# A convolution on one Trainium2 core: all input loads issued at the start, the first store held until the sixth of seven has landed

## The chip, the core and the metric

The kernel runs on one core of a Trainium2 chip. The time is device microseconds of one execution, given as the median of several runs. Before the change it is 125.88 us, the median of three runs (125.75 to 125.93).

## What is computed

```python
x: (16, 64, 64, 64) float32        # batch, c_in, h, w
weight: (128, 64, 3, 3) float32    # 90% of its entries are zero
x_pad = pad(x, 1 pixel of zeros on each side of h and w)
output[b, co] += weight[co, ci, kh, kw] * x_pad[b, ci, kh:kh+64, kw:kw+64]   # over ci, kh, kw
```

It is an ordinary 3x3 convolution with padding 1. The output is (16, 128, 64, 64) float32. The kernel uses the weights as a dense matrix. HBM gives 16.78 MB of x and 0.29 MB of weights, and takes 33.55 MB of output; the profile counts 17.07 MB read and 33.55 MB written.

## The kernel before

**Pairs.** The 16 images are worked on in eight pairs, p = 0 to 7. A pair's two images lie on 128 partitions (2 x 64 input channels) in one bf16 tile `xs[p]` of 64 x 64 pixels. All eight tiles stay in SBUF. The loads run on POOL's DMA queue (L63 and `load`, L68) and cast float32 to bf16 on the way, so a full load reads 2.10 MB of HBM and writes 1.05 MB into SBUF; the profile lists it as 1024 KB. Only the upper 32 rows of pair 0 come differently: SP's queue loads them as float32 into `x_head` (L62), and DVE and ACT cast them (L101). The weights are the first transfer of SP's queue (L60).

**Work on a pair.** A pair is cut into four blocks of 16 rows. Except for the very first block (`direct`), a block goes through `twos` (L166). POOL adds each even row to the odd row below it (`s`, L169, a pool of three buffers). PE multiplies that sum (6 matmuls; L150), and ACT copies the product out of PSUM into `pc` (L176). Then PE computes what the even rows lack (12 matmuls), and DVE adds it to `pc` and writes the result into the output tile `o` (L183, two instructions), then the same for the odd rows. PSUM has eight tiles (`psum_pool`), and a block uses six of them. The two images' matmuls run on different halves of the array.

**Outputs.** `o` is a tile of 128 x 2 x 64 x 64 float32 (4.19 MB, one pair of output images), from a pool of three buffers. SP's queue stores a whole pair when its last block is done (L207), and pair 7 in two halves (L205). Pair 3 writes into the buffer of pair 0, pair 4 into that of pair 1, and so on, so DVE's first write of pair p waits for the store of pair p-3 to land.

**Order.** The schedule is by hand (`tc.manual_schedule()`): each engine does its instructions in the order of the program, and the framework adds the waits on semaphores. POOL's order counts twice, since its loads and its additions `s` are in one stream. Before the change POOL issues, ahead of its first `s`, the tail of pair 0, pairs 1 to 3 and the first 24 rows of pair 4. The rest follows behind the last block of a pair:

```python
EARLY, CUT = 4, 24
LATER = {2: (5,), 3: (6,), 4: (7, 0, 32), 5: (7, 32, 64)}
```

After pair 1 comes the rest of pair 4 (L197), after pair 2 pair 5, after pair 3 pair 6, after pairs 4 and 5 the two halves of pair 7 (L199). After the store of pair 1, SP issues five transfers of 4 bytes (`spare`, L211). Their data is never used; each takes the next semaphore of the eight that SP's transfers use in turn.

Of the kernel before, what the change touches and what calls it, by code (L numbers as in the profile page):

```python
# [8 lines left out]
FP32 = mybir.dt.float32  # L9
# [2 lines left out]
SUB = mybir.AluOpType.subtract  # L12

BLOCKS = {p: "TTTT" for p in range(8)}
BLOCKS[0] = "DTTT"  # L20


G0, G1, G2, G21, G01 = range(5)
# [4 lines left out]
def kernel(  # L28
# [6 lines left out]
    nc = tc.nc  # L35

    B, C_IN, H, W = x.shape
    C_OUT, _, KH, KW = weight.shape
    assert (B, C_IN, H, W) == (16, 64, 64, 64) and (C_OUT, KH, KW) == (128, 3, 3)
    NP = B // 2  # L40
    HEAD = 32

    const_pool = ctx.enter_context(tc.tile_pool(name="const", bufs=1))
    x_pool = ctx.enter_context(tc.tile_pool(name="x", bufs=1))
    s_pool = ctx.enter_context(tc.tile_pool(name="s", bufs=3))
    p_pool = ctx.enter_context(tc.tile_pool(name="pc", bufs=4))
    o_pool = ctx.enter_context(tc.tile_pool(name="o", bufs=3))
    psum_pool = ctx.enter_context(
        tc.tile_pool(name="psum", bufs=8, space=bass.MemoryType.PSUM)
    )  # L50
# [4 lines left out]
    def pair(p):  # L55
        return x[2 * p : 2 * p + 2].rearrange("n i h w -> (n i) h w")

    xs = [x_pool.tile([128, H, W], BF16, name=f"x{p}") for p in range(NP)]
# [5 lines left out]
    ident = const_pool.tile([128, 128], BF16, name="ident")  # L64
    make_identity(nc, ident)

    def load(p, a=0, b=H):
        nc.gpsimd.dma_start(out=xs[p][:, a:b, :], in_=pair(p)[:, a:b, :])  # L68

    EARLY, CUT = 4, 24

    LATER = {2: (5,), 3: (6,), 4: (7, 0, 32), 5: (7, 32, 64)}
    for p in range(1, EARLY):
        load(p)
    load(EARLY, 0, CUT)


    idle_rhs = const_pool.tile([128, 512], BF16, name="idle_rhs")  # L80
    nc.vector.memset(idle_rhs, 0.0)  # L81
# [2 lines left out]
    def keep_busy(n):  # L84
        for _ in range(n):
            nc.tensor.matmul(idle_ps, idle_rhs[:, 0:128], idle_rhs, start=True, stop=True)  # L86

    keep_busy(7)

    w_v = w_sb.rearrange("o (i k) -> o k i", k=KH * KW)
# [66 lines left out]
    def direct(p, o, r0, rows):  # L159
        ps = product(  # L160
            [(xs[p], G1, r0, 1), (xs[p], G0, r0 - 1, 1), (xs[p], G2, r0 + 1, 1)], rows
        )
        nc.scalar.copy(out=o[0][:, r0 : r0 + rows, :], in_=ps[0])  # L163
        nc.vector.tensor_copy(out=o[1][:, r0 : r0 + rows, :], in_=ps[1])  # L164

    def twos(p, o, r0):  # L166
        t0 = r0 // 2
        s = s_pool.tile([128, 8, W], BF16, name="s")
        nc.gpsimd.tensor_tensor(  # L169
            out=s, in0=xs[p][:, r0 : r0 + 16 : 2, :], in1=xs[p][:, r0 + 1 : r0 + 16 : 2, :], op=ADD  # L170
        )
        shared = product([(s, G1, 0, 1)], 8)
        pc = []
        for n in range(2):
            c = p_pool.tile([128, 8, W], FP32, name="pc")
            nc.scalar.copy(out=c, in_=shared[n])  # L176
            pc.append(c)
        even = [(xs[p], G21, r0 + 1, 2), (xs[p], G0, r0 - 1, 2)]
        odd = [(xs[p], G01, r0, 2), (xs[p], G2, r0 + 2, 2)]
        for first, terms in ((r0, even), (r0 + 1, odd)):  # L180
            ps = product(terms, 8)
            for n in range(2):
                nc.vector.tensor_tensor(  # L183
                    out=o[n][:, first : r0 + 16 : 2, :], in0=ps[n], in1=pc[n], op=ADD
                )

    for p in range(NP):
        both = o_pool.tile([C_OUT, 2, H, W], FP32, name="o")
        o = [both[:, n] for n in range(2)]
        into = out[2 * p : 2 * p + 2].rearrange("n o h w -> o n h w")  # L190
        last = p == NP - 1
        for blk in range(4):
            r0 = 16 * blk
            if BLOCKS[p][blk] == "T":
                twos(p, o, r0)
                if p == 1 and blk == 3:
                    load(EARLY, CUT, H)  # L197
                elif blk == 3 and p in LATER:
                    load(*LATER[p])  # L199
            else:  # L200
                for r, rows in ((r0, 8), (r0 + 8, 8)):
                    direct(p, o, r, rows)
            if last and blk % 2 == 1:
                rows = slice(r0 - 16, r0 + 16)
                nc.sync.dma_start(out=into[:, :, rows, :], in_=both[:, :, rows, :])  # L205
        if not last:
            nc.sync.dma_start(out=into, in_=both)  # L207
        if p == 1:
            spare = const_pool.tile([1, 5], FP32, name="spare")
            for k in range(5):  # L210
                nc.sync.dma_start(out=spare[:, k : k + 1], in_=weight[0:1, 0, 0, 0:1])  # L211


# [28 lines left out]
```

## Time and profile before

| | |
|---|---|
| time, median of 3 runs | 125.88 us (125.75 to 125.93) |
| span of the profiled execution | 124.3 us, so 1.5 us of the time lie outside the span |
| PE busy | 108.7 us (87%) |
| DVE busy | 82.5 us (66%) |
| ACT and POOL busy | 39.0 and 41.7 us |
| shares of the 16 DMA engines: SP's queue q1, POOL's queue q0 | 67.2% and 30.7% |
| stores issued by SP (pairs 0 to 6, then the two halves of 7) | 23.03, 35.78, 48.58, 61.39, 74.19, 87.00, 99.81; 106.16 and 112.61 us |

The profile shows one execution, in microseconds from the first instruction. A page of it gives the busy time of each engine, rows of 40 slices for engines and DMA, the queues, the chain of work that ended last, the groups of instructions, and the DMA issues with their time to landing. "SPq" and "POOLq" are the DMA queues that SP and POOL fill: q1 (called hardware_dynamic) and q0 (software_dynamic). "Landing" is when the transfer's semaphore reports it complete.

One column needs care. The bytes of q0 are those written into SBUF as bf16. A casting load reads twice as many bytes from HBM, so q0's megabytes are doubled below wherever a rate at the HBM is meant.

### The profile page before, as it was taken

Reading aid. Unit: us, or ns where it says so; the run is one execution under the profiler, and the core shown is the slowest. Engines: PE = TensorE matmul, PEld = TensorE weight load, DVE = VectorE, ACT = ScalarE, POOL = GpSimd, SP = SyncE. Lnnn points to the kernel's source line nnn. Section 1 sums busy time; section 2 is a strip of 40 time slices with the busy share of each in tenths; the row PEclk is TensorE's granted clock in tenths of the full one; section 3 lists DMA queues with packets and bytes.
Section 4 is the critical chain, followed back from the end, with each engine's and each line's share of the span. In section 5 each row is a group of like instructions: output and inputs, shape, how many; then the busy total and the mean of one; then the engine's idle time right before and its main releaser. Section 6 shows DMA issues by size and latency. Waiting matters only on the chain.

```text
span 124.3 us, 2453 instructions
## 1 busy us (share of the span) xinstructions
PE 108.7 (87%) x989; PEld 57.2 (46%) x989; DVE 82.5 (66%) x135; ACT 39.0 (31%) x71; POOL 41.7 (34%) x47
## 2 busy tenths in 40 slices
PE   6959999999999999999999999999999999970000
PEld 2425555555555555555555555555555555530000
DVE  0353577877787778777877878887877787772000
ACT  4543333333333333333333333333333333330000
POOL 6409333533353335333443335333333320000000
PEclk9999999999999999999999999999999999997555
DMA  4999999999999999999999999999999999999991
GB/s 120 348 220 227 219 213 213 238 411 338 335 392 422 319 316 324 377 340 329 303 385 378 354 380 443 376 349 389 418 422 437 422 427 427 437 427 403 432 414 82
DMA packets 4198, 42.91 MB, mean 345 GB/s; under 512 B 347, under 2 KB 347, under 8 KB 1115
## 3 DMA queue, kind: packets, MB, share of 16 engines
q1 hardware_dynamic: 2746, 34.90, 67.2%
q0 software_dynamic: 1440, 7.86, 30.7%
q8 instruction: 7, 0.11, 0.3%
q14 instruction: 5, 0.03, 0.1%
HBM read 17.07 MB, written 33.55 MB: 407 GB/s over the span
## 4 chain that ended last, share of the span: by engine, by line
PE 82%; DMA 5%; DVE 1%; issue 1%; DVEq 0%; SPq 0%
PE ps L150 82%; DMA x_head<-in_x_dram 5%; DVE o L183 1%; DVEq L237 0%; DVE x L101 0%; SPq L60 0%; DVEq L183 0%
## 5 line engine op out<-in xcount | busy, mean ns | idle before, releaser
L183 DVE TENSOR_TENSOR o<-ps,pc 128x512 f32<-128x512 f32 x124 | 77.8, 686 | 22.1 <-PE ps L150 19.2
L150 PE MATMUL ps<-x,wT 64*128 64x504 bf16 (+3 forms) x780 | 88.8, 373 | 1.3 <-DVE x L101 1.3
L150 PEld LDWEIGHTS <-wT 64*128 64x128 bf16 x966 | 55.2, 94 | 49.5 <-issue 1.7
L169 POOL TENSOR_TENSOR s<-x 128x512 bf16<-128x512 bf16 x31 | 35.6, 1150 | 57.6 <-PE ps L150 41.1
L176 ACT COPY pc<-ps 128x512 f32<-128x512 f32 x62 | 33.3, 589 | 64.0 <-issue 61.8
L150 PE MATMUL ps<-s,wT 64*128 64x512 bf16 (+1 forms) x186 | 25.7, 377 | 0.0
L86 PE MATMUL ps<-idle_rhs 128*128 128x512 bf16 x14 | 4.8, 505 | 1.2 <-DVE idle_rhs L81 1.2
L68 POOL DMA_DIRECT2D x<-in_x_dram x9 | 5.0, 560 | 0.0
L86 PEld LDWEIGHTS <-idle_rhs 128*128 128x128 bf16 x14 | 1.5, 118 | 3.2 <-issue 1.4
L105 DVE CAST w_bf<-w_sb 128x192 bf16<-128x192 f32 (+1 forms) x4 | 1.1, 351 | 2.5 <-DMA w_sb<-in_weight_dram 2.5
L164 DVE COPY o<-ps 128x512 f32<-128x512 f32 x2 | 1.4, 692 | 2.0 <-PE ps L150 2.0
L101 DVE CAST x<-x_head 128x576 bf16<-128x576 f32 x1 | 0.5, 460 | 2.6 <-DMA x_head<-in_x_dram 2.6
L101 ACT CAST x<-x_head 128x576 bf16<-128x576 f32 (+1 forms) x2 | 1.5, 802 | 1.8 <-DMA x_head<-in_x_dram 1.8
L163 ACT COPY o<-ps 128x512 f32<-128x512 f32 x2 | 1.2, 586 | 2.4 <-PE ps L150 2.4
L105 ACT ACT_TABLE_LOAD x1 | 1.3, 1283 | 0.7 <-PEq L226 0.7
L105 ACT CAST w_bf<-w_sb 128x64 bf16<-128x64 f32 (+1 forms) x2 | 0.7, 416 | 1.6 <-DMA w_sb<-in_weight_dram 1.6
L115 DVE TENSOR_TENSOR wT<-ps,wT 128x384 bf16<-128x384 f32 x2 | 1.0, 548 | 0.0
L111 PEld LDWEIGHTS <-w_bf 128*128 128x128 bf16 x9 | 0.5, 97 | 1.0 <-DVE w_bf L105 1.0
L63 POOL DMA_DIRECT2D x<-in_x_dram x1 | 0.7, 693 | 0.8 <-POOLq L226 0.8
L111 PE MATMUL ps<-ident,w_bf 128*128 128x128 bf16 x9 | 0.9, 222 | 0.1
L81 DVE MEMSET idle_rhs<- 128x256 uint32 x1 | 0.3, 272 | 0.9 <-PEq L226 0.9
L126 DVE CAST wT<-ps 128x384 bf16<-128x384 f32 x1 | 0.6, 551 | 0.0
(8 smaller groups left out, 1.9 us busy)
## 6 DMA issues: line engine op xcount, KB each, us to landing
out_dram<-o SPq DMA_DIRECT2D x7, 4096.0 KB, 19.8
x<-in_x_dram POOLq DMA_DIRECT2D x5, 1024.0 KB, 16.8
out_dram<-o SPq DMA_DIRECT2D x2, 2048.0 KB
x<-in_x_dram POOLq DMA_DIRECT2D x3, 512.0 KB, 13.8
x_head<-in_x_dram SPq DMA_DIRECT2D x1, 1024.0 KB, 6.2
x<-in_x_dram POOLq DMA_DIRECT2D x1, 640.0 KB, 14.8
x<-in_x_dram POOLq DMA_DIRECT2D x1, 384.0 KB, 22.3
w_sb<-in_weight_dram SPq DMA_DIRECT2D x1, 288.0 KB
```

Source lines behind the costliest of these rows:

```text
L68: nc.gpsimd.dma_start(out=xs[p][:, a:b, :], in_=pair(p)[:, a:b, :])
L86: nc.tensor.matmul(idle_ps, idle_rhs[:, 0:128], idle_rhs, start=True, stop=True)
L101: copy(out=xs[0][:, a:b, :], in_=x_head[:, a:b, :])
L105: copy(out=w_bf4[:, g, a:b, :], in_=w_v[:, k : k + b - a, :])
L111: nc.tensor.matmul(wps[:, j, :], src, ident, start=True, stop=True)
L115: nc.vector.tensor_tensor(out=wT[:, g], in0=wps, in1=wT[:, G1], op=SUB)
L150: nc.tensor.matmul(ps[n][:, lo:hi, c_lo:c_hi], tap(g, kw, n), src[q, a:b:step, c_lo + kw - 1 : c_hi + kw - 1], start=(i == 0), stop=(i == ...
L163: nc.scalar.copy(out=o[0][:, r0 : r0 + rows, :], in_=ps[0])
L164: nc.vector.tensor_copy(out=o[1][:, r0 : r0 + rows, :], in_=ps[1])
L169: nc.gpsimd.tensor_tensor(out=s, in0=xs[p][:, r0 : r0 + 16 : 2, :], in1=xs[p][:, r0 + 1 : r0 + 16 : 2, :], op=ADD)
L176: nc.scalar.copy(out=c, in_=shared[n])
L183: nc.vector.tensor_tensor(out=o[n][:, first : r0 + 16 : 2, :], in0=ps[n], in1=pc[n], op=ADD)
```

## The change

The loads of pairs 1 to 7 are all issued at the beginning, each as one transfer, and none later. The store of the first half of pair 0 additionally waits for the load of pair 6 (`loads[5]`, the sixth of the seven). The stores of pairs 0 and 1 are cut into halves, as that of pair 7 was. The three output buffers become three named tiles, used in turn. Three spare transfers remain of five.

```diff
+HALVES = (0, 1, 7)
+GATE = 6
+SPARES = 3
...
-    o_pool = ctx.enter_context(tc.tile_pool(name="o", bufs=3))
+    o_pool = ctx.enter_context(tc.tile_pool(name="o", bufs=1))
...
-    EARLY, CUT = 4, 24
-    LATER = {2: (5,), 3: (6,), 4: (7, 0, 32), 5: (7, 32, 64)}
-    for p in range(1, EARLY):
-        load(p)
-    load(EARLY, 0, CUT)
+    loads = [
+        nc.gpsimd.dma_start(out=xs[p], in_=pair(p)) for p in range(1, NP)
+    ]
...
+    outs = [o_pool.tile([C_OUT, 2, H, W], FP32, name=f"o{k}") for k in range(3)]
+    first_store = None
     for p in range(NP):
-        both = o_pool.tile([C_OUT, 2, H, W], FP32, name="o")
+        both = outs[p % 3]
...
                 twos(p, o, r0)
-                if p == 1 and blk == 3:
-                    load(EARLY, CUT, H)
-                elif blk == 3 and p in LATER:
-                    load(*LATER[p])
...
-            if last and blk % 2 == 1:
+            if p in HALVES and blk % 2 == 1:
                 rows = slice(r0 - 16, r0 + 16)
-                nc.sync.dma_start(out=into[:, :, rows, :], in_=both[:, :, rows, :])
-        if not last:
+                store = nc.sync.dma_start(out=into[:, :, rows, :], in_=both[:, :, rows, :])
+                if first_store is None:
+                    first_store = store
+                    tc.add_manual_dep(store.ins, loads[GATE - 1].ins.name, ...)
+        if p not in HALVES:
             nc.sync.dma_start(out=into, in_=both)
         if p == 1:
-            spare = const_pool.tile([1, 5], FP32, name="spare")
-            for k in range(5):
+            spare = const_pool.tile([1, SPARES], FP32, name="spare")
+            for k in range(SPARES):
```

On PE and ACT nothing moves. DVE's instructions stay in their order too; from pair 3 on, some of its additions also wait on DVE's own count, and the first write into each half of the buffers of pairs 0 and 1 waits for that half's store. On POOL the seven loads stand together ahead of the first `s`. On SP the order is: weights, `x_head`, the four half stores of pairs 0 and 1, three spares, five whole stores, two half stores.

More of the change, by code (lines that the diff above doesn't have):

```diff
@@ L65 @@
     make_identity(nc, ident)
-    def load(p, a=0, b=H):
-        nc.gpsimd.dma_start(out=xs[p][:, a:b, :], in_=pair(p)[:, a:b, :])
-    EARLY, CUT = 4, 24
-    LATER = {2: (5,), 3: (6,), 4: (7, 0, 32), 5: (7, 32, 64)}
-    for p in range(1, EARLY):
-        load(p)
-    load(EARLY, 0, CUT)
+    loads = [
+        nc.gpsimd.dma_start(out=xs[p], in_=pair(p)) for p in range(1, NP)
+    ]
     idle_rhs = const_pool.tile([128, 512], BF16, name="idle_rhs")
@@ L185, in twos @@
                 )
+    outs = [o_pool.tile([C_OUT, 2, H, W], FP32, name=f"o{k}") for k in range(3)]
+    first_store = None
     for p in range(NP):
-        both = o_pool.tile([C_OUT, 2, H, W], FP32, name="o")
+        both = outs[p % 3]
         o = [both[:, n] for n in range(2)]
         into = out[2 * p : 2 * p + 2].rearrange("n o h w -> o n h w")
-        last = p == NP - 1
         for blk in range(4):
@@ L202 @@
                     direct(p, o, r, rows)
-            if last and blk % 2 == 1:
+            if p in HALVES and blk % 2 == 1:
                 rows = slice(r0 - 16, r0 + 16)
-                nc.sync.dma_start(out=into[:, :, rows, :], in_=both[:, :, rows, :])
-        if not last:
+                store = nc.sync.dma_start(out=into[:, :, rows, :], in_=both[:, :, rows, :])
+                if first_store is None:
+                    first_store = store
+                    tc.add_manual_dep(
+                        store.ins,
+                        loads[GATE - 1].ins.name,
+                        mybir.DependencyInfo(
+                            mybir.DependencyClass.Sync, mybir.DependencyReason.DATA
+                        ),
+                        reason="loads first",
+                    )
+        if p not in HALVES:
             nc.sync.dma_start(out=into, in_=both)
         if p == 1:
-            spare = const_pool.tile([1, 5], FP32, name="spare")
-            for k in range(5):
+            spare = const_pool.tile([1, SPARES], FP32, name="spare")
+            for k in range(SPARES):
                 nc.sync.dma_start(out=spare[:, k : k + 1], in_=weight[0:1, 0, 0, 0:1])
```

## The prediction

> **What bounds the kernel now.** I read the page's rows of slices first: which resource has no free slice?
>
> ```profile
> DMA  4999999999999999999999999999999999999991
> ...
> HBM read 17.07 MB, written 33.55 MB: 407 GB/s over the span
> ```
>
> The DMA engines are busy at 90% or more in every slice but the first and the last. Next comes the chain that ended last, in order of time (start, us, what).
>
> ```profile
> 7.95 102.09 PE ps L150 x954
> ...
> 111.99 0.60 DVE o L183
> ```
>
> PE works without a pause from 7.95 to 110.04, and DVE ends at 112.59. That is 11.7 us ahead of the span's end at 124.3, and the chain does not explain them. SP's own waits do (us in total, times, longest):
>
> ```profile
> SPq L237 <- DMA out_dram<-o: 10.0, 3, 4.8
> ```
>
> SP issues the last half store at 112.61 (0.37 us) and then waits 10.0 us for stores, until about 123.0; 1.3 us of closing follow. That half is 2.10 MB, some 5 us of transfer, so it stands behind older stores. The end is set by the DMA engines, and they by the bytes: 50.63 MB through HBM. PE sets only the earliest possible end. The last three stores (pair 6 and two halves, 8.39 MB) can't begin before pair 6 is done, at 99.81. A transfer's first bytes move 1.0 us after its issue (weights: issued 0.74, DMA row non-zero from 1.75). With 8.39 MB at 429 GB/s (19.6 us) that makes 120.4. **The change can gain 123.0 - 120.4 = 2.6 us at most** while PE's schedule stays.
>
> Is the DMA time all needed? I compare three stretches by queue (packets, MB, share). First 8 to 23 us, loads alone:
>
> ```profile
> q0 software_dynamic: 463, 3.21, 102.6%
> ```
>
> Then 24 to 88 us, loads and stores mixed:
>
> ```profile
> q1 hardware_dynamic: 1244, 19.17, 71.5%
> q0 software_dynamic: 781, 3.94, 30.0%
> ```
>
> Then 92 to 121 us, stores alone:
>
> ```profile
> q1 hardware_dynamic: 1050, 12.34, 100.0%
> ```
>
> With q0 doubled: loads alone 6.42 MB in 15 us, 428 GB/s; mixed 19.17 + 7.88 = 27.05 MB in 64 us, 423; stores alone 12.34 MB in 29 us, 426. A window cuts packets at its edges, so I take landings as a second measure. These are the issues of load 3 (at 3.53) and of the store of pair 4 (at 74.19), with us to landing:
>
> ```profile
> x<-in_x_dram POOLq DMA_DIRECT2D x1, 1024.0 KB, 20.6
> ```
>
> ```profile
> out_dram<-o SPq DMA_DIRECT2D x1, 4096.0 KB, 19.8
> ```
>
> Load 3 lands at 24.1; by then 8.68 MB are done (weights 0.29, pair 0 2.10, three loads of 2.10). Pair 4's store lands at 94.0; by then all 17.07 MB of loads and five stores (20.97 MB) are done. So the mixed part moves 29.36 MB in 69.9 us, 420 GB/s. The rest, 12.58 MB of stores, goes from 94.0 to 123.0, 434 GB/s. Mixed is slower than unmixed by 0.7% (423 against 426) to 3% (420 against 434).
>
> **The change, part by part.**
>
> *Loads first, stores behind.* No byte is added or removed. After load 3 (24.1) there remain 50.63 - 8.68 = 41.95 MB; before takes 98.9 us for them (424 GB/s). Unmixed at 426 they take 98.5 (gain 0.4), at 428 98.0 (gain 0.9), at 434 96.7 (gain 2.2). A loss below nothing I put at 0.2, the coarseness of the windows. I take 429 GB/s, between the loads' 428 and the middle of 426 and 434: 97.8 us, a **gain of 1.1 us**; both ends stay for the range.
>
> *The gate.* At 429 GB/s a load takes 4.9 us, so loads 4, 5, 6 land at 29.0, 33.9, 38.8. SP stands at the first half store until 38.8. Queued behind it are three half stores, three spares and store 2. The half stores are ready (pair 1 ends at 35.78), so four issues of 0.4 us go out by 40.4 and three spares of 0.5 us by 41.9; store 2 is due at 48.58. Nothing on SP is late. The DMA engines don't run dry: load 7 has 4.9 us to run when load 6 lands, and the first store's bytes come 1.0 us after its issue. Without that cover the gate would cost about 1 us. Load 7 and the first half store still mix, 4.2 MB: at 420 instead of 429 that is 0.2 us, inside the choice above.
>
> *Output buffers.* Here the gate adds a wait: pair 3 writes into pair 0's buffer. DVE's additions after pair 2, in order of time:
>
> ```profile
> 49.14 2.53 DVE L183 TENSOR_TENSOR o<-ps,pc 128x512 f32<-128x512 f32 x4 [0.58 <-ACT pc L176]
> ```
>
> Before, store 0 (issued 23.03, 17.0 to landing) was home at 40.0, 9 us early. Now its first half lands when loads 4 to 7 and it are through: 5 x 2.10 = 10.49 MB after 24.1, at 48.5; slack 0.6 us. At 420 it is 49.1, slack nothing. The second half lands at 53.4 and is wanted two blocks later (2 x 3.2) at 55.6. Pair 1's halves land at 58.3 and 63.2, wanted at 62.0 and 68.4. Store 2 lands at 73.0, wanted at 74.75, slack 1.7; store 3 at 82.8, wanted at 87.6. Were a half late by a microsecond, DVE would wait, but PE has other PSUM tiles to fill: four of eight hold block 0, the other four take the next shared product and the next even one, some 2 us of work. DVE idles 0.7 us per block and catches up. Halves are what makes it fit: a whole store 0 would land at 53.4, 4.3 us too late. I cost this at nothing.
>
> *Issues on POOL.* Four loads now take 2.15 us ahead of the first `s`; seven take 3.8:
>
> ```profile
> 2.46 2.15 POOL L68 DMA_DIRECT2D x<-in_x_dram  x4
> ...
> 9.04 3.37 POOL L169 TENSOR_TENSOR s<-x 128x512 bf16<-128x512 bf16 x3 [4.43 <-ACT x L101]
> ```
>
> POOL is done at 6.3 and `s` waits until 9.04 for ACT's cast, so the addition costs nothing; without that cover it would be 1.6 us, and the slack of 1.6 would take that (the first `s` ends at 9.04 + 1.15 = 10.19, PE reads it at 11.76). Five issues of 0.57 us between later blocks go; POOL was idle there for 2 us a block.
>
> *Two more stores, two fewer spares, DVE's waits on itself.* SP waits most of its time, so two issues of 0.4 us and two spares of 0.5 us cost nothing. DVE's count is long past when it is asked for; at the 0.04 us of issue that the chain lists ahead of a DVE instruction they lie in its idle 0.7 us per block, and at the end the last half store, issued at 112.6, stands behind stores that run until 121.9 - 4.9 = 117.0.
>
> The Trainium skill, "DMA: Bandwidth & Descriptors", section "Issuing engines are not separate DMA queues", speaks against the change: transfers of all issuing engines run on the same 16 DMA engines and interleave. By that alone the order of the same bytes is worth nothing, and the sum would be 125.9. The trace's 423 and 420 GB/s mixed against 426 to 434 unmixed say that interleaving is not quite free.
>
> The same page, "Anatomy of one DMA — SWDGE (gpsimd) path", gives each transfer a fixed 2.0 us; by it, an estimate, two more transfers would cost 4 us and give 128.8. The trace's two halves of pair 7 follow each other at 425 to 434 GB/s without a dip, so queued behind others that price is hidden.
>
> **Sum.** Against the profiled execution: stores end at 123.0 - 1.1 = 121.9, above PE's floor of 120.4; span 123.2. The median of the runs is the span plus 1.5, so I predict 125.9 - 1.1 = **124.8 us**. Its own range is 123.3 (the floor) to 125.6.
>
> **Rivals.**
>
> *Mixing costs nothing.* The 1% between windows is their edges, and the 420 is a start-up of the first store, which comes again behind the gate. For it: 423 against 426 is within what edges do. Against it: two measures with one sign. Gain -0.2 to 0.2: **125.9 us.** A gate that in fact holds nothing back belongs here too, since then mixing goes on.
>
> *POOL is held at its issues (slower).* Before never has more than five casting loads under way (the tail of pair 0, 1 to 3, a piece of 4); now there are eight. If only five may be outstanding, load 5 waits for the tail of pair 0 (1.24 + 7.8 = 9.0), load 6 for load 1 (13.9), load 7 for load 2 (3.01 + 16.3 = 19.3). The first `s` starts at 19.9, 10.8 us late, less 1.6 of slack: PE stands 9.2 us, the floor goes to 129.6, and the time to 125.9 + 6.6 = **132.5 us**. With six allowed, POOL is free at 14.5, PE stands 3.8 us, and the time is 127.1. It decides as soon as PE stands more than 2.6 us, that is, POOL is held past 13.2. Against it: the fifth issue took no longer than the first (0.54 to 0.57 us).
>
> *A buffer comes home late (slower).* To lose, PE must stand over 2.6 us, so the first half store must land some 5 us after 49.1; each us beyond costs one. At a landing of 55, **127 us.** Nothing in the rates gives that.
>
> **How the numbers follow.** A measurement here can tell about 0.2%, 0.25 us, from no change. Forecast (123.3 to 125.6) 0.74; mixing free 0.13; POOL held 0.07; late buffer 0.06. So faster 0.74, same 0.13, slower 0.13. The range takes in forecast and no change: 123.3 to 126.2, leaving out the slower cases.
>
> **What would show it.** Right: the GB/s row near 215 (q0 alone) until about 39 us, then 425 to 435 to the end; first store issue at 38 to 40; last landing near 121.9; PE's work unbroken from 8 to 110. Wrong: a POOL L68 group much longer than 0.57 us each; a DVE L183 wait on DMA near 49 or 75; a DMA row below 9 after 39; stores alone no faster than 423 GB/s.

## The result and the profile after

The changed kernel takes 127.49 us (median of 4 runs, 127.32 to 128.50) against 125.85 us before (125.75 to 125.93). The ratio is 1.0144, with an interval of 1.0104 to 1.0183. It is **slower by 1.4%**. The forecast was 124.8 us, faster by 0.9%, and the time lies outside its range of 123.3 to 126.2. The four executions of the changed kernel have spans of 125.5 to 125.7 us. In a later series of 19 runs on one chip, the kernel before has a median span of 124.0.

First the two rows of the page of after, DMA share and rate in 40 slices:

```profile
DMA  4999999999999999999999999999999999999960
GB/s 130 345 222 219 216 211 211 216 222 214 216 214 209 271 415 425 422 433 417 435 433 438 422 433 417 433 430 428 422 449 422 420 417 433 428 409 428 425 295 13
```

The forecast's picture is there. The rate stays near 215 (loads alone, counted as written) until slice 13, then 409 to 449 (stores alone) until the last two slices, and no slice but the first and the last two is below 9. Issues on POOL and on SP are as worked out (start, us):

```profile
2.47 3.73 POOL L68 DMA_DIRECT2D x<-in_x_dram  x7
8.58 3.36 POOL L159 TENSOR_TENSOR s<-x 128x512 bf16<-128x512 bf16 x3 [2.38 <-ACT x L91]
```

```profile
38.94 2.99 SPq L192 DMA_DIRECT2D out_dram<-o  x4
41.98 2.41 SPq L208 DMA_DIRECT2D spare<-in_weight_dram  x3
```

And PE is not late either. From the chain of after, in order of time:

```profile
7.50 102.09 PE ps L140 x954
...
110.86 0.68 DVE o L173
```

PE works 102.09 us without a pause, to the hundredth as before, and ends at 109.59, 0.45 earlier than before. So nothing that the forecast feared has happened: POOL is not held, and no output buffer stops PE. The end is late all the same. SP's waits:

```profile
SPq L234 <- DMA out_dram<-o: 11.7, 3, 4.8
```

They were 10.0 us; SP now waits 11.7. What for shows in the DMA rows of the last stretch, 122.8 to 124.4 us, in slices of 0.04 us:

```profile
DMA  0000004000000040000000400000040000000000
...
q1 hardware_dynamic: 5, 0.03, 4.9%
```

Five packets are left (four of 8 KB and one of 4 bytes that reports them), and they come one after the other, 0.3 us apart. That is one DMA engine of sixteen at work and fifteen that are done. The trace's packet records give, for the last half store, when each of the 16 engines reports its part (us):

```
before  121.0 121.0 121.0 121.1 121.3 121.3 121.5 121.9 122.1 122.3 122.3 122.4 122.5 122.8 122.9 123.0
after   120.6 120.7 120.7 120.8 121.1 121.2 121.3 122.1 122.1 122.1 122.2 122.3 122.4 122.6 122.6 124.3
```

Fifteen engines are done at 122.6; before, fifteen are done at 122.9, 0.3 us later. The sixteenth ends 1.7 us behind them, and the kernel's end with it.

The packet records also say where it falls behind. A whole store is 16 packets of 16 KB for each engine. Of those that start between 66 and 108 us in after (1092), 997 take 609 to 619 ns. 72, one in fifteen, take 628 to 700, mostly 644, and they follow each other end to start:

```
start 96.01 96.64 97.29 97.93 98.57 ...    took 634 667 644 644 653 ns   (one engine)
```

One engine is 5% slower than the others: a whole store takes it 10.3 us, the others 9.7. It is the one that ends last: with the stores of pairs 4, 5 and 6 it is through 0.7, 1.3 and 1.7 us after the other fifteen, and from then on the distance stays. The slow packets begin near 45 us, when the loads are through. They end at 111, just after PE's end at 109.6. Before shows such a run on one engine too, from 88.8, when its loads are through, to 111.4 (the records don't number the engines, so whether it is the same one is not known). With 102 packets (two of 8 KB counted as one), 33 ns too long each, in after and 35 in before, the engine loses 3.4 us in after and 1.2 in before. The difference of 2.2 is the size to be explained. The last engines of the two kernels end 1.3 us apart (124.3 against 123.0). The rest is in part the 0.3 us that the other fifteen gain, in part where the engine stood among the others when its lag began, which is not worked out here.

### The profile page after: what moved, and what is told of

The parts are those of the page before. It is cut to its first block, busy times and chain, and to the rows that moved or that the text cites. A ratio compares the mean times of both kernels' runs of the same rounds, so it can differ in the third digit from the quotient of the medians.

```text
span 125.7 us, 2489 instructions
## 1 busy us (share of the span) xinstructions
PE 109.4 (87%) x989; PEld 57.2 (46%) x989; DVE 82.3 (65%) x135; ACT 39.0 (31%) x71; POOL 40.7 (32%) x45
## 4 chain that ended last, share of the span: by engine, by line
PE 81%; DMA 5%; DVE 1%; issue 1%; DVEq 1%; SPq 0%
PE ps L140 81%; DMA x_head<-in_x_dram 5%; DVE o L173 1%; DVEq L234 0%; DVE x L91 0%; SPq L60 0%; DVEq L173 0%
## 5 line engine op out<-in xcount | busy, mean ns | idle before, releaser
L140 PE MATMUL ps<-x,wT 64*128 64x504 bf16 (+3 forms) x780 | 88.8, 373 | 0.2 <-DVE x L91 0.2
L140 PEld LDWEIGHTS <-wT 64*128 64x128 bf16 x966 | 54.8, 94 | 48.7 <-issue 0.4
L77 PE MATMUL ps<-idle_rhs 128*128 128x512 bf16 x14 | 5.3, 541 | 1.2 <-DVE idle_rhs L72 1.2
L68 POOL DMA_DIRECT2D x<-in_x_dram x7 | 3.7, 561 | 0.0
L63 POOL DMA_DIRECT2D x<-in_x_dram x1 | 0.7, 696 | 0.8 <-POOLq L223 0.8
L114 ACT CAST wT<-ps 128x384 bf16<-128x384 f32 x1 | 0.5, 478 | 0.3 <-PE ps L101 0.3
```

The lines of the kernel that those rows point to most:

```text
L68: nc.gpsimd.dma_start(out=xs[p], in_=pair(p)) for p in range(1, NP)
L140: nc.tensor.matmul(ps[n][:, lo:hi, c_lo:c_hi], tap(g, kw, n), src[q, a:b:step, c_lo + kw - 1 : c_hi + kw - 1], start=(i == 0), stop=(i == ...
```

## The experiments

**Theory 1:** while stores run alone beside PE's work, one DMA engine lags, and the change lengthens that stretch from 22 to 66 us. **Theory 2:** the cost lies in the handover from loads to stores and in the half stores. **Theory 3:** output buffers come home late. Ratios are against the kernel before in the same series; times in brackets are the ratio times 125.85 us.

### The parts of the change

**Loads alone** (e1): the kernel before, with

```diff
-    for p in range(1, EARLY):
-        load(p)
-    load(EARLY, 0, CUT)
+    for p in range(1, NP):
+        load(p)
```

and the later loads removed.

> The kernel before with one edit: all seven casting loads issued at the start, whole; no gate, whole stores, five spares. Theory 1 (one lagging DMA engine: while stores run without loads beside PE's work, one of the 16 engines takes 644 ns per 16 KB packet where the others take 611, and the stores' end waits for it): loads and stores mix from 23 to about 62 us, stores run alone from 62 to 111, 27 us more than before's 22, so the engine falls 1.4 us further behind, less some 0.5 us for the shorter mixed stretch: 126.7 us. Theory 2 (the change's cost is the handover from loads to stores at the gate plus the 8 KB packets of the half stores): neither is here, 125.9 us. Theory 3 (late output buffers): 125.9 us.

Measured: 1.0065, 1.0032 to 1.0098 (126.7 us), as theory 1 has it. The last engine ends 1.1 us behind the others (123.8 against 122.7). A second cost shows as well. The first store, issued at 22.62, moves its first bytes only at 26.6, and the rate sags meanwhile. Before, the first store finds only the end of one piece queued and moves at 24.3, 1.3 us after its issue. The queues in the window 24 to 28 us:

```profile
q0 software_dynamic: 73, 0.59, 90.5%
q1 hardware_dynamic: 14, 0.23, 13.7%
```

That is 2 x 0.59 + 0.23 = 1.41 MB in 4 us, 353 GB/s where loads alone reach 428: 0.7 us of DMA time lost, once. (Such a row counts a packet where it starts; with packets shared out over the window's edges it is 0.8.) PE also stands 1.4 us near 65, behind DVE, but the DMA engines have work queued all the while.

**No gate** (e2): the changed kernel with `GATE = 0` and `if GATE and first_store is None`.

> The changed kernel without its gate: the first half store waits for its data alone. Theory 1 (lagging engine): stores start at about 17 us and mix with loads until about 60 to 65; stores alone for some 48 us beside PE's work, against 67 in the changed kernel and 22 before: 126.7 us. Theory 2 (handover at the gate and half stores): the handover goes, the halves stay (four half stores at 16 packets of 315 ns against 8 of 617, 0.1 us each): 126.2 us. Theory 3 (late buffers): no lateness without the gate, 125.9 us.

Measured: 1.0122, 1.0064 to 1.0180 (127.4 us). Theory 1's 126.7 lies at the lower edge, theory 2's 126.2 below it. The gate is not what costs: without it the time is that of the changed kernel within the intervals. Stores alone last from 57 to 111 us here, and the last engine is 1.5 us behind the next (124.1 against 122.6), much as in after.

**Whole stores of pairs 0 and 1, with the gate** (e3): `HALVES = (7,)`, the wait moved to the whole store of pair 0.

> The changed kernel with whole stores of pairs 0 and 1 (and five spares); loads first and gate as in the changed kernel. Pair 3 must now wait for the whole store of pair 0, which lands near 54 us where 49 is wanted, so PE stands 2 to 3 us. Theory 1 (lagging engine): PE's end is not what ends last, the engine is; stores alone last 2 us longer beside PE's work: 127.3 to 127.6 us. Theory 2 (handover and half stores): without the 8 KB packets 0.4 us less than the changed kernel, 127.1 us. Theory 3 (late buffers): PE's standing comes on top, 129.5 to 130.5 us.

Measured: 1.0272, 1.0210 to 1.0333 (129.3 us). Theory 3 comes nearest, and its wait is there. DVE after pair 2:

```profile
55.34 4.99 DVE L173 TENSOR_TENSOR o<-ps,pc 128x512 f32<-128x512 f32 x8 [7.07 <-DMA out_dram<-o]
```

It waits 7.07 us for the whole store; PE ends at 116.8, the DMA engines run empty later, and all sixteen end within 0.2 us of each other. So the half stores do what the forecast said they do: in after DVE's first write of pair 3 comes at 50.00 instead of 48.7, 1.3 us late, and PE feels nothing.

**Halves alone** (e4): the kernel before, `if p in (0, 1, 7)` for the half stores, three spares.

> The kernel before with one edit: pairs 0 and 1 stored in halves (three spares); loads as before, no gate. Theory 1 (lagging engine): loads stay spread until 89 us, stores alone last 22 us as before; 125.9 us, at most 0.2 more. Theory 2 (handover and half stores): the half stores' share alone, 126.2 to 126.4 us. Theory 3 (late buffers): buffers come home no later than before, 125.9 us.

Measured: 1.0077, 1.0042 to 1.0111 (126.8 us). No theory gave this much; theory 2 came nearest. The queues in 15 to 24 us, where the first half store joins three queued loads:

```profile
q0 software_dynamic: 195, 1.47, 84.3%
q1 hardware_dynamic: 74, 0.61, 16.5%
```

2 x 1.47 + 0.61 = 3.55 MB in 9 us, 394 GB/s, again a sag of 0.7 us. All engines end later, and none stands out (the last two both at 123.4).

**One pair in halves** (e10: `p in (1, 7)`; e11: `p in (0, 7)`; four spares each).

> The kernel before with pair 1 alone stored in halves (pair 0 whole, so the first store is issued at 23 us as before). Theory A (a store that joins a queue full of loads costs 0.5 to 1 us of DMA time once; half stores of pair 0 do so since they start at 16 us, with three loads still to come): the first store joins as before, 125.9 us. Theory B (8 KB packets of half stores are the cost): half of the 0.9 us that both pairs' halves cost, 126.3 us.

> The kernel before with pair 0 alone stored in halves (pair 1 whole), so the first store is issued near 16 us, with three loads still queued. Theory A (joining a full queue of loads costs): nearly all of the 0.9 us that both pairs' halves cost, 126.6 us, and the rate at the HBM between 15 and 24 us falls to about 400 GB/s. Theory B (8 KB packets): half of it, 126.3 us.

Measured: e10 1.0069, 1.0036 to 1.0103 (126.7 us); e11 1.0057, 1.0022 to 1.0092 (126.6 us). e11 agrees with theory A (126.6), and its rate between 15 and 24 us sags as in e4:

```profile
q0 software_dynamic: 192, 1.44, 84.4%
q1 hardware_dynamic: 69, 0.57, 15.4%
```

That is 3.45 MB, 383 GB/s. e10 agrees with neither: its first store starts 1.0 us after its issue, as soon as before's does, and it costs as much. In the execution whose packets are kept, the longest of twelve, one engine ends 1.3 us behind the next (125.0 against 123.7); it is as far behind near 95 us already, so this is not the growing lag of after. The costs of the two pairs don't add up to e4's either. That half stores cost 0.6 to 0.8% on the kernel before is measured; that a store which joins queued loads is one reason is shown; the rest stays open.

**Gate at the seventh load** (e12): `GATE = 7`.

> The changed kernel with the gate at the seventh load: the first store waits until all loads have landed, near 43.5 to 45 us, so nothing mixes at all. Theory A (stores joining loads cost by the joining): no joining, but the DMA engines stand for 1 to 3 us between the last load and the first store, while the changed kernel loses 0.5 us there; so 0.5 to 2 us more than the changed kernel, 128.0 to 129.5, and pair 3 waits for its buffer (first half store lands near 51, wanted at 49). Forecast's view (the handover is covered, unmixed is better): 127.5 us or less.

Measured: 1.0314, 1.0245 to 1.0384 (129.8 us), a little above theory A's range. The DMA row from 40 to 48 us:

```profile
DMA  7997997790540300000000096891988979969879
```

The engines stand nearly still from 42.8 to 44.6 us, and DVE waits 5.2 us for buffers, in three waits. So the gate at the sixth load is rightly placed, and the cover of the seventh is needed. Unmixing fully is not better.

### What slows the one engine

**Few matmuls** (e5), the changed kernel with

```diff
-        todo = [(t, kw) for t in terms for kw in KW_ORDER]
+        todo = [(t, kw) for t in terms for kw in KW_ORDER][:1]
```

> The changed kernel with only the first matmul of each product for either image (6 of 30 per block; the other taps are left out, so the output is not the convolution). DVE's, ACT's and POOL's work stays. Theory 1a (the lagging DMA engine is slowed by PE's work, its instructions or its data): its 16 KB packets take nearer to 611 than 644 ns while stores run alone, about 618, and the last transfer ends with the others, near 122.7 instead of 124.35 us. Theory 1b (it is slowed by DVE's and ACT's traffic): it stays at 644 ns until DVE ends, near 97 to 100 us, and lands near 123.9. Rival (that engine is slow by itself, whatever runs): 644 ns to the end, landing near 124.6 or later.

**No additions** (e6): `range(2 if p < 3 else 0)` around DVE's addition.

> The changed kernel without DVE's additions from pair 3 on (the output tiles of pairs 0 to 2 are stored again in their place, so the output is not the convolution). PE, ACT and POOL work as before. The stores no longer wait for data. Theory 1a (PE's work slows the engine): packets stay at 644 ns until PE ends near 109, last landing 124.2 us. Theory 1b (DVE's traffic): 611 to 620 ns after 46 us, last landing near 122.7. Rival (slow by itself): 644 to the end, 124.6 or later.

**Stores only** (e7): nothing computed for `p >= 3`.

> The changed kernel without any computation from pair 3 on (the output tiles of pairs 0 to 2 are stored again, so the output is not the convolution): loads, then stores alone with all engines idle after about 47 us. Theory 1 (one DMA engine is slowed beside computation): 611 ns packets on every engine after 47 us, no straggler, last landing near 122.5 us. Rival (slow by itself): one engine at 644 ns to the end, last landing 125 us.

Measured, one execution each: spans 123.6, 124.8 and 124.0 us.

- Without DVE's additions the slow packets stay (67 of 1096 between 66 and 108 us, until 110.5), the engine takes 10.3 and 10.1 us for two whole stores, and it ends 1.1 us behind the others, at 123.4. It is not DVE's traffic.
- Without any computation they are gone: 3 of 1104. One engine is 1.1 us behind when computing stops, near 47 us, and it is still 1.1 behind at the end: 9.7 us for every store. No engine is slow by itself. Here the expected last landing of 122.5 came at 122.8.
- With a fifth of the matmuls, few slow packets come, mostly of 634 ns, and the last landing is 122.3 us, 0.4 behind the others.

So PE slows it, and the next run is about what of PE.

**Small matmuls** (e9), e7 with these in place of each block of the later pairs:

```diff
+    def tiny(n):
+        t = psum_pool.tile([128, 512], FP32, name="ps")
+        for _ in range(n):
+            nc.tensor.matmul(t[:, 0:64], idle_rhs[:, 0:128], idle_rhs[:, 0:64], start=True, stop=True)
...
+            if p >= 3:
+                tiny(30)
```

> The kernel without computation from pair 3 on, but with 30 matmuls of 64 columns in place of each block's 30 of 512 (idle operands; all else of these pairs is left out, so the output is not the convolution). PE has the same number of instructions there, with an eighth of the data. Theory 1c (the lagging DMA engine is slowed by the number of PE's instructions): while the small matmuls run, from about 47 us on, its 16 KB and 8 KB packets take 644 and 325 ns, as in the changed kernel or more, and they fall to 611 and 309 when PE ends; it ends later than with stores alone (122.8) by up to 2 us. Theory 1d (by the data PE reads): 611 to 618 ns throughout, last landing 122.8 us.

Measured: span 124.5 us, last landing 123.2. PE in order of time:

```profile
46.73 6.53 PE L82 MATMUL ps<-idle_rhs 128*128 128x64 bf16 x218
55.06 3.91 PE L82 MATMUL ps<-idle_rhs 128*128 128x64 bf16 x128 [1.80 <-issue]
61.53 5.29 PE L82 MATMUL ps<-idle_rhs 128*128 128x64 bf16 x128 [2.56 <-issue]
```

and the 8 KB packets of the slow engine beside them (the others take 309 ns):

```
start 50.28 50.64 51.00 51.38 51.74         took 361 361 380 371 361 ns        PE busy
start 53.53 53.84 54.15 54.45 54.76 55.07   took 313 309 309 309 309 313 ns    PE pausing
start 55.38 55.73 56.09 56.46 56.83         took 361 361 380 371 361 ns        PE busy again
```

The engine is slow when PE issues and quick when PE pauses, 53.3 to 55.1 us. 218 matmuls and as many weight loads in 6.53 us are 67 instructions per us; 954 and as many in 102.09 us are 19, in the changed kernel. That is 3.6 times as many, and the slowing is 20% (371 against 309) instead of 5.3% (644 against 611), 3.8 times as much. A later burst of 128 in 5.29 us, 48 instructions per us, lies between them: 342 ns, 11%. **The slowing follows the number of PE's instructions**, and theory 1c's forecast came. It is not the data that the matmuls stream: at 128 x 64 elements each instead of 64 x 500 they read 0.9 times as much per us as in the changed kernel. The weights are not ruled out: each load here is 128 x 128 instead of 64 x 128, seven times as much per us.

**The change without PE's instructions** (e13 and e14): the edit of e5 on both kernels, timed.

> The kernel before with only the first matmul of each product (6 of 30 per block; the other taps are left out, so the output is not the convolution). Control for the next run. Theory 1 (one DMA engine is slowed by the number of PE's instructions, most where stores run alone): before has only 22 us of stores alone, and its last engine leads the next by 0.1 us only, so little is gained: span 123.6 to 124.0 against 124.05 with all matmuls. Theory 2 (the change's cost is in the handover, the half stores and the order of transfers, whatever PE does): 123.5 to 124.0 too; the two differ in the comparison with the next run.

> The changed kernel with only the first matmul of each product (the other taps are left out), timed this time. Theory 1: with a fifth of PE's instructions the lagging engine keeps pace with the others in the 67 us of stores alone, and the change costs nothing any more: span 123.5 to 123.9 against 125.5 with all matmuls, and from 0.3 us above to 0.3 below the kernel before with few matmuls. Theory 2: the change still costs about 1.5 us over the kernel before with few matmuls, span 125 to 125.5.

Measured: e13 1.0008, 0.9980 to 1.0036 (median span 124.35); e14 0.9983, 0.9964 to 1.0002 (median span 123.85). e13's span is 0.35 us above what was expected. e14's is within, but its gain over e13 is 0.2 us more than was expected at most. The question is their difference. With all matmuls the change costs 1.5 us of span (125.5 against 124.0). With a fifth of them it **gains 0.5 us** (123.85 against 124.35). Theory 2 wanted 1.5 us of cost to stay. So some 2.0 us of the change's cost hang on PE's instructions, against the 2.2 worked out from the packets. Of the 2.0, 1.65 are the changed kernel's gain; 0.35 is a loss of the kernel before, which no run explains.

One rival is settled by the records. With fewer matmuls the DMA engines also carry less for the queue that the page calls instruction. In after and in e14:

```profile
q8 instruction: 7, 0.11, 0.3%
```

```profile
q8 instruction: 1, 0.02, 0.0%
```

But only four of the seven packets come after 45 us, where the lagging engine has the worth of 102 long ones. And while three of them pass (at 71.0, 84.9 and 98.9 us, 0.9 us each) the lagging engine's own packets go on end to start. Another engine carries them.

**Relief for the engine** (e8): pair 7's first half store cut by partitions into 0 to 119 and 120 to 127.

> The changed kernel with the first half store of pair 7 cut in two by partitions, 0 to 119 and 120 to 127: the first piece divides by fifteen and not by sixteen, so one DMA engine gets none of it, and the small piece goes to eight engines. Whether the engine left out is the lagging one is not known beforehand. Theory 1 (the end waits for the lagging engine): if it is the one left out, it loses 16 packets of 8 KB, 4.9 us, and the end falls to the next engine, 122.7 to 123.3 us instead of 124.35: 125.9 to 126.4 us in time. If it is another engine, the end stays or rises by 0.6 us: 127.5 to 128.1. Theory 2 (cost spread over all engines, by handover and half stores): 127.5 us or slightly more in either case.

Measured: 1.0520, 1.0483 to 1.0557 (132.4 us): it failed for a reason of its own. The queue in 112 to 122 us, with packets and MB, of an execution that was itself longer than the median:

```profile
q1 hardware_dynamic: 373, 2.88, 97.6%
```

2.88 MB in 10 us where after moves 3.99. The 8 KB packets take 444 ns on average where after's take 310; half of them take 309 as elsewhere, and a quarter 600 or more. Why is not known, and it tells nothing on theory 1.

## Why the prediction was wrong

**The failed step is the sum over "the DMA engines" as one pool:** "Unmixed at 426 they take 98.5 (gain 0.4) ... I take 429 GB/s ... 97.8 us, a gain of 1.1 us". The rate is right: in after, stores alone move this much in 62 to 110 us,

```profile
q1 hardware_dynamic: 1356, 20.53, 100.5%
```

20.53 MB in 48 us, 428 GB/s. But the end is the end of the last engine, and that one does not run at the pool's rate. While stores run alone beside PE it needs 644 ns for a packet where the pool needs 611. In the mixed stretches of before most take 624 and the rest nearly all 611; packets of 628 or more are rare (22 of 778 from 45 to 88 us). For the engine that ends last, mixing is 3% quicker than not mixing: the sign of the change's main term is turned. The second measure, 434 GB/s for stores alone by landings (94.0 to 123.0), misled for a like reason: a landing, too, is that of the last engine. When pair 4's store landed at 94.0, the engines that were through with it had already moved 0.66 MB of the next ones; by the packet records 11.92 MB and not 12.58 went from 94.0 to 123.0, and the last 2 us of that are thin, since the engines end one by one.

- **The gain of unmixing** is real for the pool but smaller than 1.1: fifteen engines end 0.3 us earlier, and without most of PE's instructions the kernel gains 0.5. By the packet records before moves 424 GB/s from 45 to 89 us, and 418 from 24 to 45, where its queues join; at 428 the same bytes would take some 0.9 us less. The joining behind the gate takes 0.5 to 0.7 of that back. The first rival said that the joining comes again behind the gate, and that was right; that mixing costs nothing was wrong, and it did not foresee the loss.
- **"The DMA engines don't run dry", "bytes come 1.0 us after its issue"**: the first store is issued at 38.94, and its first packets move at 42.1, 3.2 us later. The window 40 to 45 us in after:

```profile
q0 software_dynamic: 70, 0.46, 51.3%
q1 hardware_dynamic: 113, 0.93, 44.4%
```

  That is 1.85 MB where 429 GB/s would move 2.15: a loss of 0.7 us (0.5 with packets shared out over the window's edges), costed at 0.2.
- **Buffers:** mechanism and halves right; the first half came 1.0 us after its forecast (49.5 instead of 48.5), and PSUM's spare tiles hid it as said. Store 2 was late by 0.7 us at 74.41, hidden too.
- **POOL and SP's issues:** right to 0.2 us. The rival "POOL is held" is out.
- **Two more stores "cost nothing":** measured on the kernel before, 0.6 to 0.8%. How much of it is in the changed kernel no run separates: with few matmuls the whole change, halves included, gains. The prediction's estimate of 4 us for them took a figure that its page gives for transfers issued from GpSimd; these are SP's, and the whole change cost 1.6.

## What to carry to other kernels

A transfer that is spread over sixteen DMA engines ends with the slowest of them: read how far apart the engines end, not only what they move together. Here loads beside the stores hid a lagging engine, and taking them away let it show. Where a kernel is bound by its DMA engines, a new order of the same bytes has to be worth more than the price of letting two queues join, 0.5 to 0.9 us each time here.

## What the runs showed of the hardware that was not expected

- One DMA engine slows with the number of PE's instructions: 16 KB packets of stores take 644 ns instead of 611 at 19 instructions per us, and 8 KB packets 371 instead of 309 at 67; without PE it keeps pace. What it carries for PE, no run shows (not the packets of the instruction queue, as said above); nor whether it does so in an execution that is not recorded, since every run here has its record. The Trainium skill, "DMA: Bandwidth & Descriptors", section "Latency and other measured facts", knows two engines as usually slower and takes, as a best guess, the descriptors of transfers issued from GpSimd for the cause. Here one engine lags while no such transfer is under way (45 to 111 us), so that guess does not cover this case; whether it is one of those two the records don't tell.
- A queue that joins another with work outstanding starts late: 1.0 us with idle engines (the weights), but 3.2 us (after), 3.8 (e2, e4, e11) and 4.0 us (e1) for a store behind queued loads. The rate sags meanwhile, to 353 GB/s over 4 us in e1.
- Cutting one half store into 120 and 8 partitions cost 4.9 us (132.4 against 127.5). The one execution whose packets are kept, some 3 us longer than the median, moves 288 GB/s from 112 to 122 us where the changed kernel moves 399; why is not known.
